# Input projection of a two-layer transformer trunk: chunks in pairs on four accumulators, with seven block products for some K pairs

## The chip, the cores and the metric

The kernel runs on one core of a Trainium2 chip. The metric is the device time of one execution in microseconds (us). The kernel before takes 2220.35 us, the median of 3 runs (2220.18 to 2223.35).

## The reference

Two layers, 256 tokens, width 2048, all float32:

```python
for l in range(DEPTH):
    h = rms_norm(x, pre_mix_norm[l])
    # hybrid_mixer: proj = h @ w_in[l]          (2048 -> 6144)
    #   columns: stick-breaking q, k, v (8 heads x 128),
    #            differential q, k (8 x 2 x 64), v (8 x 128)
    #   A: stick-breaking attention, RMSNorm per head
    #   B: differential attention (two softmax maps, partial rotary on q and k), RMSNorm per head
    #   mix = concat(A, B);  m = mix @ w_o[l]    (2048 -> 2048)
    x = x + rms_norm(m, post_mix_norm[l])
    h = rms_norm(x, pre_ffn_norm[l])
    f = (silu(h @ w_gate[l]) * (h @ w_up[l])) @ w_down[l]   # 2048 -> 5632 -> 2048
    x = x + rms_norm(f, post_ffn_norm[l])
```

## The kernel before

Tokens lie on the 128 partitions in NT = 2 tiles (t = 0, 1). Every weight matrix is cut into chunks of CW = 512 columns and into K pairs (`kp`), that is 2 x 128 rows; one K pair of one chunk is a weight tile of 128x1024 float32, 512 KB. All weight tiles form one stream (`weight_order`), which `fetch` loads on SyncE's queue in that order into "raw" buffers (4 of them), and `feed` splits on the way: ScalarE (ACT) rounds to `hi` (L229), VectorE (DVE) subtracts to `lo` (L231), 6 buffers each. `weights(i, ahead)` keeps the split LOOKAHEAD = 4 tiles ahead of use. The activations are held split too (`xT`, or `xI` in layer 1: one tile per 128 rows, two halves). A **product** of a 128x128 block of activations with a 128x512 block of weights is three matmuls: hi x hi, hi x lo, lo x hi (`unit`, L414 to L416; `product`, L774 to L776).

The stages of a layer are input projection, attention, output projection, gate/up and down projection. In the input projection, `mixer_in` goes through 12 chunks one by one. A chunk takes 2 of the 4 PSUM banks of tag "acc", one for each token tile; the next chunk takes the other two. Chunk number c stands for `kind, g = divmod(c, 2)`: kinds 0, 1, 2 are q, k, v of the stick-breaking heads, kinds 3, 4, 5 those of the differential heads, g is the half of the heads. The order is 6, 8, 10, 7, 9, 11, then 0, 2, 4, 1, 3, 5: the differential heads first. The output projection then reads the mixed heads in the order of `KP_O`, again the differential ones first, and waits with `run_until` for the ones that it needs. When a chunk is done, ACT scales it by the inverse RMS `rs` into `tok` or `v`; POOL rotates differential q and k; `flip` transposes tok on TensorE (PE) through a bank of tag "b" (3 banks), and DVE copies it out (L748). Then `diff_weights` or `stick_weights` compute the attention weights through "b" banks, and `attend` multiplies them with v in the one bank of tag "o". These are generators; `tick()`, called at the start of each group of matmuls, lets them take their next step, so attention's instructions fall between matmuls of the projection. `run_until` ticks until a condition holds. Above that, a scheduler orders each engine's instructions by priority and expected readiness; `tc.high_priority(offset=URGENT)` moves a part forward.

Layer 0 begins with `opening`: x arrives transposed in 8 loads (`xr`), is scaled, split into `xT`, and used at once. `settle` then loads x again, in token order, for its mean squares (`inv_rms`), and loads the small constants (`late_constants`). Layer 1's `xT` is written by the end of layer 0: the down projection's last three K pairs run token tile by token tile, and `rescale` transposes x column group by column group.

Gate/up and down already use **seven products** for some K pairs (`seven_products`; of gate/up's 8, the list SEVEN = 2, 4, 5, 6): the 2x2 block product of (2 token tiles x 2 row blocks) with (2 row blocks x 2 chunks) takes 8 products when done directly; with sums of the operands prepared beforehand it takes 7, four of them into extra banks (`four_banks`), whose contents `shared_part` combines (one ACT copy, four DVE adds). The sums of the weights are made by `mixed_weights`: the tile `T` gets one sum from an accumulating DMA of POOL's queue (`summed`, L191), then DVE makes three adds (L210 to L212) and splits all of it (L206: lo, and Tl in two parts, one 128x512 and one 128x1024). The sums of the activations are made by `token_sums`, from the pair's plain values `f`.

Of the kernel before, what the change touches and what calls it, by code (L numbers as in the profile page):

```python
# [9 lines left out]
F32 = mybir.dt.float32  # L10
# [7 lines left out]
P = 128  # L18
# [12 lines left out]
DEFER = 8  # L31
# [3 lines left out]
KP_O = (4, 5, 6, 7, 0, 1, 2, 3)  # L35
SEVEN = (2, 4, 5, 6)
# [15 lines left out]
def weight_order():  # L52
# [8 lines left out]
    sevens = set()  # L61
    for l in range(L):
        lay = {"in": {}, "o": {}, "gate": {}, "up": {}, "down": {}}
        chunks = []
        for g in range(2):
            chunks += [6 + g, 8 + g, 10 + g]
        for g in range(2):
            chunks += [g, 2 + g, 4 + g]
        lay["chunks"] = chunks
# [21 lines left out]
    return order, plan, sevens  # L91
# [14 lines left out]
class Rooms:  # L106


    LASTING = ("gpost", "t2", "x", "qk")

    def __init__(self, tc, name):
        self.lasting = tc.alloc_tile_pool(name=f"{name}_lasting", bufs=6, reuse_waits="tile")
        self.passing = tc.alloc_tile_pool(name=f"{name}_passing", bufs=6, reuse_waits="tile")

    def tile(self, *args, **kw):
        return (self.lasting if kw["tag"] in self.LASTING else self.passing).tile(*args, **kw)

    def release(self):
        self.passing.release()
        self.lasting.release()  # L120
# [3 lines left out]
def kernel(  # L124
# [35 lines left out]
    order, plan, sevens = weight_order()  # L160
# [35 lines left out]
    def mixed_weights(i):  # L196
# [10 lines left out]

        split(hi, lo, u)
# [10 lines left out]
    def feed(upto):  # L219
        fetch(upto)  # L220
        while fed[0] < min(upto, len(stream)):
            i = fed[0]
            raw = raws[i]
            if i in sevens:
                ready[i] = mixed_weights(i)
                fed[0] += 1
                continue
# [145 lines left out]
    def inv_rms(t, pool, nm):  # L373
        ss = small.tile([P, 1], F32, tag="ssx", name=f"ssx_{nm}_{t}")
        part = small.tile([P, 4], F32, tag="ssp", name=f"ssp_{nm}_{t}")
        for h in range(4):
            junk = pool.tile([P, CW], F32, tag="t2", name=f"junk_{nm}_{t}_{h}")
            nc.scalar.activation(junk, x_part(t, h * CW, CW), AF.Square, accum_out=part[:, h : h + 1])
# [7 lines left out]
    running = []  # L386

# [63 lines left out]
    def norm_pair(pool, ob, mix, mixed, h0, gcol, nm):  # L451
# [10 lines left out]
        )  # L462
        yield
        yield
        for j in range(2):
            mix[h0 + j] = pool.tile([P, 2, S], F32R, tag="mix", bufs=KT, name=f"mix_{nm}_{j}")
# [38 lines left out]
    def stick_weights(pool, l, g, st):  # L505
        q, k = st["q"], st["k"]
        for hp in range(2):
            nm = f"sb{l}_{g}_{hp}"
            za, zb = bank(f"za_{nm}"), bank(f"zb_{nm}")
# [36 lines left out]
            w = pool.tile([P, 2 * (S + P)], F32, tag="w", bufs=3, name=f"w_{nm}")  # L546
            nc.scalar.activation(w[:, 0 : 2 * S], za, AF.Exp)
            nc.scalar.activation(w[:, 2 * S : 2 * S + S], zb[:, 0:S], AF.Exp)
            yield
            yield  # L550
# [7 lines left out]
    def diff_weights(pool, l, g, st):  # L558
        q, k = st["q"], st["k"]
        for hp in range(2):  # L560
            w = pool.tile([P, 2 * (S + P)], F32, tag="w", bufs=3, name=f"pT_{l}_{g}_{hp}")
            for j in range(2):
                h = 2 * hp + j
                nm = f"df{l}_{g}_{h}"
                sc = [bank(f"s{m}_{nm}") for m in range(2)]
                for qt in range(2):
                    for m in range(2):
                        r = slice(m * 64, (m + 1) * 64)
                        nc.tensor.matmul(
                            sc[m][:, qt * P : qt * P + (qt + 1) * P],  # L570
                            q[r, h, qt * P : (qt + 1) * P],
                            k[r, h, 0 : (qt + 1) * P],
                            start=True,
                            stop=True,
                        )
                mx = small.tile([P, 4], F32, tag="mx", name=f"mx_{nm}")
                for m in range(2):
                    blk = sc[m][0:64, 0 : S + S].rearrange("p (b c) -> p b c", c=64)[:, 1:6:4, :]
                    nc.vector.memset(blk, NEG)
                    for qt in range(2):  # L580
                        nc.vector.tensor_reduce(
                            out=mx[:, 2 * qt + m : 2 * qt + m + 1],
                            in_=sc[m][:, qt * P : qt * P + (qt + 1) * P],
                            axis=AX.X,
                            op=ALU.max,
                            negate=True,
                        )
                yield
                e = pool.tile([P, 2, S + P], F32, tag="a", bufs=2, name=f"e_{nm}")
                sm = small.tile([P, 4], F32, tag="sm", name=f"sm_{nm}")  # L590
                for m in range(2):
                    for qt in range(2):
                        c = 2 * qt + m
                        nc.scalar.activation(
                            e[:, m, qt * P : qt * P + (qt + 1) * P],
                            sc[m][:, qt * P : qt * P + (qt + 1) * P],
                            AF.Exp,
                            bias=mx[:, c : c + 1],
                            accum_out=sm[:, c : c + 1],
                        )  # L600
# [37 lines left out]

    def opening(pool, accs, xT):

        first = plan[0]["chunks"][0]

        xr = []

# [451 lines left out]
```

## Time and profile before

| | |
|---|---|
| median of 3 runs | 2220.35 us (2220.18 to 2223.35) |
| profiled execution | 2224.29 us, its span 2222.6 us |
| granted TensorE clock, mean | 0.997 |
| busy: PE / DVE / ACT / POOL | 2197.2 / 1790.0 / 1307.7 / 135.1 us |
| input projection, layer 0 | matmuls from 6.1 to 308.2 us |
| input projection, layer 1 | matmuls from 1107.8 to 1410.5 us |
| DMA | 464.65 MB, mean 209 GB/s |

The profile is of one execution. Busy time of PE is the time in which at least one matmul is under way; matmuls overlap, so it is not the sum of their durations. The granted clock is TensorE's, 1.00 being full speed. A wait is given as the engine and line that waited, and what ended the wait.

### The profile page before, as it was taken

The numbers are of one execution on the slowest core, as the hardware profiler recorded it, in microseconds if no ns is written. First come the engines' busy times: TensorE is split into PE (matmuls) and PEld (weight loads), VectorE is DVE, ScalarE is ACT, GpSimd is POOL, SyncE is SP. The second block draws the span as 40 slices with busy tenths as digits, with TensorE's granted clock in tenths as the row PEclk, the third lists the DMA queues.
The fourth block names the chain that finished last, engine by engine and source line by source line (L and its number), as shares of the span: only waits on it lengthen the run. The fifth ranks groups of instructions, "written<-read, shape, count | busy, mean of one in ns | idle before, by whom it ended". The sixth has DMA issues, their size and how long they took to land.

```text
span 2222.6 us, 28460 instructions
## 1 busy us (share of the span) xinstructions
PE 2197.2 (99%) x10057; PEld 1803.2 (81%) x10057; DVE 1790.0 (81%) x2531; ACT 1307.7 (59%) x1937; POOL 135.1 (6%) x184
## 2 busy tenths in 40 slices
PE   9999999999999999999999999999999999999998
PEld 7888888778888888888888888887788888878886
DVE  6666555899999998989876665559999999989897
ACT  6555554656656656656665455547566556566663
POOL 1200000000100000000010000000000000000000
PEclk9999999999999999999999999999999999999999
DMA  8555455777776675767464655558677677667673
GB/s 287 193 164 168 161 186 184 253 223 229 225 250 213 215 251 186 242 211 243 156 220 166 195 170 169 183 187 271 203 220 238 223 223 235 223 200 240 199 256 99
DMA packets 136783, 464.65 MB, mean 209 GB/s; under 512 B 15680, under 2 KB 16192, under 8 KB 136128
## 3 DMA queue, kind: packets, MB, share of 16 engines
q1 hardware_dynamic: 119216, 428.20, 56.0%
q0 software_dynamic: 15552, 28.32, 7.6%
q10 hardware_dynamic: 1872, 6.31, 0.7%
q8 instruction: 79, 1.29, 0.2%
q14 instruction: 64, 0.52, 0.1%
HBM read 454.38 MB, written 8.39 MB: 208 GB/s over the span
## 4 chain that ended last, share of the span: by engine, by line
PE 87%; DVE 7%; issue 2%; DMA 2%; ACT 2%; SPq 0%; DVEq 0%; ACTq 0%
PE c L774 8%; PE c L775 8%; PE c L776 8%; PE in L414 8%; PE in L416 8%; PE in L415 8%; PE dn L980 5%; PE dn L981 5%; PE dn L983 5%; PE o L416 3%; PE o L415 3%; PE o L414 2%; PE p L775 2%; PE p L774 2%; PE p L776 2%
## 5 line engine op out<-in xcount | busy, mean ns | idle before, releaser
L231 DVE TENSOR_TENSOR lo<-raw,hi 128x1024 fp32r<-128x1024 f32 x567 | 687.3, 1225 | 240.2 <-ACT hi L229 236.0
L229 ACT ACTIVATE hi<-raw 128x1024 fp32r<-128x1024 f32 x567 | 592.1, 1055 | 389.1 <-PE in L416 160.2
L774 PE MATMUL c<-hi,xF 128*128 128x512 f32 x820 | 321.8, 396 | 6.4 <-DVE w L815 2.9
L776 PE MATMUL c<-hi,xF 128*128 128x512 f32 x820 | 320.0, 392 | 0.0
L775 PE MATMUL c<-lo,xF 128*128 128x512 f32 x820 | 319.9, 391 | 0.0
L191 POOL DMA_DIRECT2D T<-in_weights_in_turn_dram x108 | 94.1, 871 | 1715.7 <-DMA T<-in_weights_in_turn_dram 540.4
L774 PEld LDWEIGHTS c<-hi,xF 128*128 128x128 f32 x820 | 154.0, 188 | 41.1 <-DVE w L815 4.1
L980 PE MATMUL dn<-hi,jh 128*128 128x512 f32 x464 | 180.8, 390 | 0.0
L776 PEld LDWEIGHTS c<-hi,xF 128*128 128x128 f32 x820 | 154.4, 188 | 32.4
L981 PE MATMUL dn<-lo,jh 128*128 128x512 f32 x464 | 180.6, 389 | 0.0
L775 PEld LDWEIGHTS c<-lo,xF 128*128 128x128 f32 x820 | 154.6, 189 | 30.8
L414 PE MATMUL in<-hi,xT 128*128 128x512 f32 x384 | 154.1, 402 | 1.6 <-ACT hi L229 1.6
L414 PE MATMUL in<-hi,xI 128*128 128x512 f32 x384 | 153.9, 401 | 0.2 <-ACT xI L355 0.2
L231 DVE TENSOR_TENSOR lo<-G,hi 128x1024 fp32r<-128x1024 f32 x108 | 131.6, 1219 | 26.5 <-ACT hi L229 26.4
L415 PE MATMUL in<-lo,xT 128*128 128x512 f32 x384 | 150.5, 392 | 0.5 <-DVE lo L231 0.5
L416 PE MATMUL in<-hi,xT 128*128 128x512 f32 x384 | 150.9, 393 | 0.0
L416 PE MATMUL in<-hi,xI 128*128 128x512 f32 x384 | 150.5, 392 | 0.1
L415 PE MATMUL in<-lo,xI 128*128 128x512 f32 x384 | 150.0, 391 | 0.5 <-DVE lo L231 0.5
L983 PE MATMUL dn<-hi,jl 128*128 128x512 f32 x464 | 142.9, 389 | 0.0
L205 ACT ACTIVATE Th<-T 128x512 fp32r<-128x512 f32 x108 | 67.7, 627 | 127.5 <-DVE T L210 127.1
L206 DVE TENSOR_TENSOR lo<-T,hi 128x1024 fp32r<-128x1024 f32 x108 | 131.6, 1219 | 12.3 <-ACT hi L205 12.2
L206 DVE TENSOR_TENSOR Tl<-G,Th 128x1024 fp32r<-128x1024 f32 x108 | 131.7, 1220 | 10.1 <-ACT Th L205 10.1
(310 smaller groups left out, 4310.4 us busy)
## 6 DMA issues: line engine op xcount, KB each, us to landing
raw<-in_weights_in_turn_dram SPq DMA_DIRECT2D x567, 512.0 KB, 4.3
T<-in_weights_in_turn_dram SPq DMA_DIRECT2D x108, 512.0 KB, 4.3
G<-in_weights_in_turn_dram SPq DMA_DIRECT2D x108, 512.0 KB, 4.6
T<-in_weights_in_turn_dram POOLq DMA_DIRECT2D x108, 256.0 KB, 6.7
away_ffn<-x ACTq DMA_DIRECT2D x8, 512.0 KB, 7.0
xd<-away_ffn SPq DMA_DIRECT2D x8, 512.0 KB, 10.3
xr<-in_x_columns_dram SPq DMA_DIRECT2D x8, 256.0 KB, 6.7
x<-in_x_dram SPq DMA_DIRECT2D x4, 512.0 KB, 8.2
```

Source lines behind the costliest of these rows:

```text
L206: nc.vector.tensor_tensor(out=l, in0=w, in1=h.bitcast(F32), op=ALU.subtract)
L229: nc.scalar.activation(hi, raw, AF.Copy)
L231: nc.vector.tensor_tensor(out=lo, in0=raw, in1=hi.bitcast(F32), op=ALU.subtract)
L414: nc.tensor.matmul(a, sh, hi[:, kk, :], start=first and kk == 0, stop=False)
L415: nc.tensor.matmul(a, sh, lo[:, kk, :], start=False, stop=False)
L416: nc.tensor.matmul(a, sl, hi[:, kk, :], start=False, stop=last and kk == 1)
L774: nc.tensor.matmul(a, sh, hi, start=first, stop=False)
L775: nc.tensor.matmul(a, sh, lo, start=False, stop=False)
L776: nc.tensor.matmul(a, sl, hi, start=False, stop=last)
L980: nc.tensor.matmul(accs[c, t], sh, hi[:, kk, :], start=first, stop=False)
L981: nc.tensor.matmul(accs[c, t], sh, lo[:, kk, :], start=False, stop=False)
L983: nc.tensor.matmul(accs[c, t], sl, hi[:, kk, :], start=False, stop=last)
```

## The change

- The 12 chunks go in 6 pairs (`PAIRS`). A pair's two chunks are computed together, K pair by K pair, on all four "acc" banks (`eight_in`: 8 products, 24 matmuls). The first and the last K pair of a pair of chunks go token tile by token tile, and after each half of the last one `settle(t)` reads two banks, with priority.
- K pairs listed in `IN_NOW` use seven products (`seven_in`), in one burst per pair of chunks: none in layer 0's first pair, 5 and 6 in layer 1's first, 4, 5, 6 in the second, 4 and 5 in the three after it, none in the last. The extra banks are the three "b" and the one "o", which attention uses otherwise. `IN_ORDER` puts the K pairs 0, 1 ahead of the burst and 2, 3, 7 behind it.
- Attention steps that take such banks start only if they end before the next burst (`clear(n)`), and one at a time (`claims`); `diff_weights` runs as two generators, one for each j.
- For these tiles the first weight sum is made by DVE on tiles loaded plainly (`plain`), not by an accumulating DMA.
- In layer 0 the opening does a pair of chunks, x for the mean squares is loaded beside it (`first_stats`), and the token sums of K pairs 4, 5, 6 are made beside it too. In layer 1 they are made during the first pair of chunks.
- The copies out of `flip` and of the transposed differential weights move from DVE to ACT. The pools are laid out anew; x for the residual is loaded in the last pair.

```diff
-DEFER = 8
+PAIRS = ((6, 8), (10, 7), (9, 0), (11, 2), (1, 3), (4, 5))
+IN_SEVEN = (4, 5, 6)
+IN_ORDER = (0, 1, 4, 5, 6, 2, 3, 7)
+IN_NOW = tuple((first, (4, 5, 6), (4, 5), (4, 5), (4, 5), ()) for first in ((), (5, 6)))
...
-        for c in chunks:
-            for kp in range(KT // 2):
-                lay["in"][c, kp] = queue_pair("w_in", l, kp, c)
+        for n, (ca, cb) in enumerate(PAIRS):
+            for kp in IN_ORDER if n else range(KT // 2):
+                lay["in"][ca, kp] = queue_pair("w_in", l, kp, ca)
+                lay["in"][cb, kp] = queue_pair("w_in", l, kp, cb)
+                if kp in IN_NOW[l][n]:
+                    plain.add(lay["in"][cb, kp])
...
+        if i in plain:
+            nc.vector.tensor_tensor(out=u[:, 0, :], in0=g[:, 0, :], in1=u[:, 0, :], op=ALU.add)
         split(hi, lo, u)
...
+    def clear(n):
+        return burst[0] is None or clock[0] + n <= burst[0]
...
         for hp in range(2):
-            while (hp, 1) not in st["w"] or "v" not in st:
+            while (hp, 1) not in st["w"] or "v" not in st or claims[1] or not clear(4):
                 yield 1
+            claims[1] += 1
...
-                nc.vector.tensor_copy(wj, tp[:, 0 : S + P])
+            nc.scalar.copy(wj, tp[:, 0 : S + P])
...
         for kp in range(KT // 2):
             if kp:
                 split(2 * kp)
                 split(2 * kp + 1)
-            if kp + 4 < KT // 2:
+            if kp + 2 < KT // 2:
                 load()
-                fetch(kp + 5)
-            unit(accs, xT, plan[0]["in"][first, kp], kp, range(NT), kp == 0, kp == KT // 2 - 1, 0)
+                fetch(2 * kp + 6)
+            for part in ((0,), (1,)) if kp == KT // 2 - 1 else (range(NT),):
+                eight_in(accs, xT, 0, PAIRS[0], kp, part, kp == 0, kp == KT // 2 - 1, 0)
+                if kp == KT // 2 - 1:
+                    settle(part[0])
+            if 3 <= kp < 7:
+                next(stats)
+            if kp >= 4 and kp - 4 < len(IN_SEVEN):
+                sums_of(IN_SEVEN[kp - 4])
...
+    def eight_in(accs, xT, l, cc, kp, toks, first, last, ahead=LOOKAHEAD):
+        ws = [weights(plan[l]["in"][c, kp], ahead) for c in cc]
+        for kk in range(2):
+            for t in toks:
+                tick()
+                st = xT[2 * kp + kk]
+                stat = (st[:, 0, t * P : (t + 1) * P], st[:, 1, t * P : (t + 1) * P])
+                for col, (hi, lo) in enumerate(ws):
+                    product(accs[2 * t + col], stat, (hi[:, kk, :], lo[:, kk, :]), first and kk == 0, last and kk == 1)
...
+        for n, cc in enumerate(PAIRS):
+            banks = [acc_bank(f"in{l}_{c}_{t}") for t in range(NT) for c in cc]
+            mine = IN_NOW[l][n]
+            w, toks = None, {}
+            def settle(t):
+                with tc.high_priority(offset=URGENT):
+                    for col, c in enumerate(cc):
+                        kind, g = divmod(c, 2)
+                        src = banks[2 * t + col]
+                        if w is not None:
+                            src = w[:, 2 * t + col, :]
+                            nc.vector.tensor_tensor(out=src, in0=banks[2 * t + col], in1=src, op=ALU.add)
...
+                        nc.scalar.activation(tok, src, AF.Copy, scale=rs[t][:, by : by + 1])
...
+                    if n == 0 and 2 <= j < 2 + len(IN_SEVEN):
+                        sums_of(IN_SEVEN[j - 2])
+                    if kp in mine:
+                        if extra is None:
+                            extra = four_banks(True, [f"{q}_in{l}_{n}" for q in ("p1", "p6", "p7", "q5")])
+                        seven_in(banks, extra, forms[kp], xT, l, cc, kp, kp == mine[0], kp == mine[-1])
+                        if kp == mine[-1]:
+                            burst[0] = None
+                            w = pool.tile([P, 4, CW], F32, tag="gpost", bufs=1, name=f"w{l}_{n}")
+                            shared_part(extra, [w[:, i, :] for i in range(4)])
...
+                    if first or last:
+                        for t in range(NT):
+                            eight_in(banks, xT, l, cc, kp, (t,), first, last)
+                            if last:
+                                settle(t)
+                    else:
+                        eight_in(banks, xT, l, cc, kp, range(NT), first, last)
```

More of the change, by code (lines that the diff above doesn't have):

```diff
@@ L637, in rotate, with opening @@
         eng.tensor_tensor(out=v16, in0=ra, in1=rb, op=ALU.add)
-    def opening(pool, accs, xT):
-        first = plan[0]["chunks"][0]
+    def opening(pool, accs, xT, stats, sums_of, settle):
         xr = []
```

380 lines of the change are left out of this document (222 added, 158 removed).

## The prediction

> **What bounds the kernel now.** I read the page's busy shares first, then the chain of waits and TensorE's own waits, then the time by stage, and last the first microseconds instruction by instruction.
>
> ```profile
> PE 2197.2 (99%) x10057; PEld 1803.2 (81%) x10057; DVE 1790.0 (81%) x2531; ACT 1307.7 (59%) x1937; POOL 135.1 (6%) x184
> ...
> PE   9999999999999999999999999999999999999998
> ...
> DVE  6666555899999998989876665559999999989897
> ...
> PE 87%; DVE 7%; issue 2%; DMA 2%; ACT 2%; SPq 0%; DVEq 0%; ACTq 0%
> ```
>
> TensorE (PE) is busy everywhere and carries 87% of the chain. VectorE (DVE) has a hole just where the change works: tenths 5 and 6 at the start and in the middle, which are the two input projections (0 to 308 us and 1107 to 1410 us), and nines elsewhere. The same by stage, in windows of 40 us (columns: stretch, length, busy us and instructions of PE, weight load, DVE, ACT, POOL, then clock, DMA share, GB/s):
>
> ```profile
> 60.00:100.00 40.00, 40.00 (x201) 31.96 (x200) 26.13 (x46) 19.17 (x35) 1.93 (x2) 1.00 0.60 200
> 260.00:300.00 40.00, 40.00 (x196) 33.46 (x195) 20.84 (x25) 18.98 (x29) 0.00 (x0) 1.00 0.58 197
> 460.00:500.00 40.00, 38.28 (x171) 30.76 (x169) 37.88 (x48) 23.86 (x29) 3.46 (x4) 1.00 0.66 200
> 600.00:640.00 40.00, 40.00 (x182) 33.06 (x181) 37.56 (x44) 23.72 (x28) 3.48 (x4) 1.00 0.72 234
> ```
>
> The first two are input projection: DVE 52 to 65%. The last two are gate/up, which has seven products already: DVE at 94% and PE without a gap once settled (600), but 1.7 us of PE lost in 40 while a backlog of DVE is being worked off (460). These two are my scale for the changed stage. PE's waits in the whole run are few:
>
> ```profile
> PE c L774 <- DVE w L815: 2.9, 2, 1.8
> PE p_d L775 <- DVE Tl L206: 2.0, 2, 1.7
> PE in L414 <- ACT hi L229: 1.6, 1, 1.6
> PE in L415 <- DVE lo L231: 1.1, 2, 0.5
> ```
>
> So the prices are: an instruction less on PE is worth its spacing, and an instruction more on DVE is free until it makes PE late. The spacing, and the one weak place of the input projection, are in PE's timeline (start, us, engine, line):
>
> ```profile
> 8.80 0.39 PE L416 MATMUL in<-hi,xT 128*128 128x512 f32 x1
> 10.79 0.73 PE L414 MATMUL in<-hi,xT 128*128 128x512 f32 x2 [1.59 <-ACT hi L229]
> 12.04 0.50 PE L415 MATMUL in<-lo,xT 128*128 128x512 f32 x1 [0.53 <-DVE lo L231]
> 13.48 0.63 PE L414 MATMUL in<-hi,xT 128*128 128x512 f32 x1
> 13.90 0.63 PE L415 MATMUL in<-lo,xT 128*128 128x512 f32 x1
> 20.35 0.39 PE L415 MATMUL in<-lo,xT 128*128 128x512 f32 x1
> 20.58 0.39 PE L416 MATMUL in<-hi,xT 128*128 128x512 f32 x1
> ```
>
> Matmuls start 0.2265 us apart (20.35 to 20.58; 29 of them from 17.40 to 23.98), although each lasts 0.39 us: the spacing counts, not the duration.
>
> **Part 1, fewer matmuls.** The list IN_NOW marks 9 K pairs in layer 0 and 11 in layer 1. Each does 7 block products in place of 8, and a product is 3 matmuls: 20 x 3 = 60 fewer; PE's instruction order of the changed kernel has 2244 matmuls of the input projection against 2304. 60 x 0.2265 = 13.6 us, all on the path. That is the ceiling of this part: **-13.6 us**.
>
> **Part 2, the opening.** Between 8.80 and 16.02 us only 12 matmuls run after the one at 8.80: 7.0 us for 2.7 us of work, 4.3 us lost, 2.1 us of it waiting for the second weight tile and 2 us because matmuls then come 0.43 us apart (the granted clock of 10 to 15 us is 0.76). With two chunks at a time a K pair feeds PE 24 matmuls (5.44 us) for 1.25 MB in place of 12 (2.72 us) for 0.75 MB. By the order of the loads, the second K pair's weights stand 0.5 to 1 MB later in the queue; at 320 to 400 GB/s (5 to 15 us) that is some 2 us later, when PE has 2.7 us more to do. I take 1.8 us lost instead of 4.3: **-2.5 us**, between 0 and -4.
>
> **Part 3, DVE's load.** Counted from the order of both kernels, over two layers: 20 Tl of 128x1024 (1.220) and 20 of 128x512 (0.684), 80 adds on raw tiles (the three that the gate/up helper has, plus the one that a DMA of POOL does there; 0.686), 36 adds of shared_part and 36 of settle (0.686), 6 token-sum sets (2 x 0.419 + 4 x 0.285 + 0.683 = 2.66): 24.4 + 13.7 + 54.9 + 49.4 + 16.0 = 158 us. Off DVE go 32 flip copies (0.686) and 16 pT copies (0.554), 31 us, to ACT, which is below 65% here. Net +127 us, 64 a layer. DVE was busy 191 us of layer 0's first 308 (sum of the windows), so it comes to about 255 of 301, 85%. Below the 94% at which gate/up runs without gaps: on the average this costs PE nothing. It costs where load is bunched.
>
> In a burst a seven needs eight DVE operations (2 lo, 4 adds, 2 Tl), 7.1 us of durations, or 6.3 us back to back (the next start follows a 128x1024 after 1.13, 1116.21 to 1117.34 us, and a 128x512 after 0.60, 1106.59 to 1107.19), and PE uses it up in 21 x 0.2265 = 4.76 us. A burst of three is 4.6 us short, one of two 3.1 us. The cover is the lead: hi and lo have 6 buffers, Th and Tl 2, so two K pairs are ready ahead, and an eight gives back 3.2 us (5.44 less 2 x 1.13). Gate/up does kp 4, 5, 6 in a row under the same cover. I cost bursts in the middle at nothing; without the lead they are the first rival.
>
> **Part 4, layer 1's first pair.** Here the load is bunched. In the trace of before DVE is full there with rescaling and transposing x, 4.6 to 5.0 of each 5 us from 1105 to 1125. The change puts behind that three token-sum sets, two sevens, shared_part and four settling adds. From the order, back to back from 1130.5 us (where the old kernel's eighth weight tile is done): the second seven's last Tl comes at about 1155, and ten of the pair's matmuls wait for it, 2.3 us more: 1157.5. PE alone would be done at 1155.5 (the old second chunk ended at 1156.9, less 6 matmuls). Then shared_part and settle end at about 1163, while PE has only 14 matmuls on the one bank already free: another 2.5 us. With half a microsecond for the next seven: **+5 us**, between 0 (the DVE sum is 5% off, or the next pair fills the gap) and 9.
>
> **Part 5, the handovers.** Four accumulators are all that the "acc" tag has, so a pair can't start until the last one is read out: 6 handovers a layer, where before two of the four were free. Covered by the split by tokens: the last K pair ends t=0 first, and its 2 banks are read (2 x 0.686) while 12 matmuls of t=1 run, 2.72 us. What DVE has just begun can cost up to 1.23 more: 2.6, still covered; one more op queued in front costs 0.5. Priority URGENT puts the reads in front. For ten of them I take 0.2 each, **+2 us**, between 0 and 8. What queues behind a late read on DVE are the next pair's lo and Tl, which have the lead.
>
> A stall can also slow the clock: after the 2.1 us of waiting at 9 to 12 us ten matmuls came 0.43 us apart, 2 us lost, while gate/up's wait of 1.8 us left the clock at 1.00. One such slow stretch in part 4 is inside its bound of 9. The page "TensorE: Matmul & The Clock Gate" of the Trainium skill (Part 1: The HAM clock gate) halves the clock only after an idle window of about 3.4 us once it is warm; by it part 4 would bring none.
>
> The handover out of layer 0's opening is another matter: rs now is computed beside it (8 squares of x on ACT behind 2 MB of loads), the lambda loads stand ahead of the next pair's weights on SP's queue, and lprod waits for them on DVE ahead of that pair's lo. Those loads take 1.3 us each on SP (32.5 to 37.7 us before). The 12.5 MB ahead of them take 39 us at 320 GB/s from 2.5, so the last x lands near 42, the weights near 47, and PE needs them at 50. **+1.5 us**, between 0 and 4.
>
> **Part 6, attention and the rest.** Same matmuls, same softmax. Steps wait for bursts to pass; PE's order shows them spread between in-projection matmuls and all scores done before the output projection, whose first 21.8 us read only differential heads (KP_O) while four reads of the stick-breaking group (some 5.5 us each) run beside. If they were late, PE would wait at the first sb K pair. 0, between -1 and 2.
>
> Sum: -13.6 - 2.5 + 5 + 2 + 1.5 = **-7.6 us**. The profiled execution took 2224.3 (span 2222.6 and 1.7 around it), 3.9 above the median of 2220.35; so 2216.7 there and **2212.7** as a median. A measurement of this kernel tells about 0.2%, 4.4 us, from no change: faster is below 2215.9, slower above 2224.8.
>
> **The rivals.**
> *The lead fails (slower).* If every seven is paced by DVE, since attention's DVE steps stand between its eight operations, each costs 6.3 - 4.76 = 1.55 us: 31 us, and with parts 1, 2 and 5 alone it is 2220.35 - 16.1 + 31 + 3.5 = 2239. It decides when DVE's share in a pair nears 95%; by my sums the pairs in the middle have 41 to 44 us of 46 to 48, 90 to 92%; from 12.6 of its 31 us on the sign turns. For: 460 to 500 us. Against: 600 to 640 us. Chance of an outcome slower than 2224.8: 0.20.
> *Handovers uncovered.* PE waits at each for two reads, 1.4 us, 12 times: 17 us in place of the 8.5 of parts 4 and 5, so 2220.35 - 16.1 + 16.8 = 2221. For: no second set of banks. Against: at the end of layer 0 the down projection's four banks pass to the next layer in the same order by tokens, and PE waited 0.2 us (1107.84). 0.13, as a result within 0.2%. The page "Perfetto Trace Analysis" of the Trainium skill (Matmuls) asks that independent groups rotate through PSUM banks, so that the reading of one overlaps the next one's matmuls; by that rule this rival is what comes.
> *All stalls vanish.* The scheduler fills layer 1's gap: -16.1 and 2 lost, 2206. 0.17.
> *My forecast*, 2207 to 2216: 0.50. That the matmuls aren't gone is excluded by the order.
>
> Faster 0.67, same 0.12, slower 0.21. The range leaves out about a tenth at each side: from 2203 (2220.35 - 13.6 - 4, the bounds of parts 1 and 2 with no stall) to 2227 (the first rival with 19 of its 31 us).
>
> **What would show it.** Right: in-projection PE count 2244; no wait of PE over 1 us from 60 to 300 us and from 1175 to 1400; DVE 80 to 92% there; PE idle of 4 to 6 us between 1145 and 1165, released by DVE Tl and w; second K pair of the opening about 2 us late at most. Wrong: many waits of about 1.5 us on Tl in each burst (first rival), waits on w or tok at each pair's first matmul (second), PE stalled at mix_sb, or gate/up later than its shift.

## The result, and the profile after

The changed kernel takes 2232.93 us, the median of 4 runs (2231.65 to 2235.65), beside 2220.54 for the kernel before in the same comparison: ratio 1.0055, 95% interval 1.0037 to 1.0072. It is 12.4 us slower; 2212.7 was forecast, 7.6 us faster. The two profiled executions lie 9.7 us apart (2233.99 and 2224.29), since the one before was 3.8 us above the median of 2220.54 and the one after 1.1.

First the page of the changed kernel: busy times, tenths of PE and DVE, and the chain's shares.

```profile
PE 2192.2 (98%) x9997; PEld 1790.3 (80%) x9997; DVE 1896.3 (85%) x2718; ACT 1363.4 (61%) x2041; POOL 137.6 (6%) x184
...
PE   9999999999999999999989999999999999999998
...
DVE  7888655899999998989899886558999999989897
...
PE 77%; DVE 13%; DMA 4%; issue 3%; ACT 2%; SPq 0%; DVEq 0%; ACTq 0%
```

The 60 matmuls are gone (x9997 against x10057). DVE has 106 us more; its first four tenths are 7 8 8 8 in place of four sixes. But PE has an 8 in the middle, where layer 1's input projection begins, and ten points of the chain have left PE, most of them for DVE and DMA. By stage (columns as before; the last row is layer 1's first pair and the beginning of the second):

```profile
60.00:100.00 40.00, 38.28 (x179) 28.98 (x178) 35.82 (x55) 26.18 (x44) 0.46 (x1) 1.00 0.58 186
260.00:300.00 40.00, 40.00 (x194) 33.45 (x193) 19.34 (x19) 21.97 (x31) 0.00 (x0) 1.00 0.56 184
1140.00:1200.00 60.00, 52.97 (x222) 39.59 (x220) 53.16 (x69) 34.55 (x42) 12.33 (x16) 0.97 0.50 160
```

In 60 us PE loses 7.0 us with DVE at 89%, less than the 94% at which gate/up ran without a gap. PE's waits (engine, line, what it waited for, then us in total, times, longest):

```profile
PE in L903 <- DVE w L794: 3.4, 1, 3.4
PE p_in L903 <- ACT Th L221: 2.7, 2, 1.6
PE qkT_ps L823 <- ACT qT L824: 2.5, 2, 1.3
PE oT_ps_df L499 <- DVE w L941: 2.3, 2, 1.2
...
PE q_in L903 <- ACT hi L221: 1.1, 1, 1.1
```

L794 is settle's add, L941 to L944 are the four adds of `shared_part`, L221 and L222 the split in `mixed_weights`, L247 and L249 the split of a plain tile, L823 and L824 the transposes of `flip` and their copy, L499 the transposes of an attention output. Two of the five are the sevens' own sums; qkT_ps and oT_ps_df are attention's transposes, for which the prediction had set nothing.

The account of the difference comes from the matmuls' start times: whatever lies between two starts beyond 0.2265 us is a gap, and the gaps above 0.34 us are put down to what stands behind them.

| in the profiled executions, us | forecast | measured |
|---|---|---|
| 60 matmuls less | -13.6 | -13.6 |
| opening, and the first matmul at 6.79 in place of 6.09 | -2.5 | -2.4 + 0.7 |
| layer 1's first pair, handover out of it included | +5 | +8.9 |
| the other handovers, and the one out of layer 0's opening | +3.5 | 0 |
| the other sevens' waits for Th, Tl and hi | 0 | +3.8 |
| attention's steps behind bursts (4.3 in layer 0, 3.4 in layer 1) | 0 | +7.7 |
| gaps under 0.34 us in the input projections | - | +2.4 |
| attention's work that moved from output to input projection | 0 | +0.6 |
| gate/up and down projection | 0 | +1.1 |
| sum | -7.6 | +9.2 |

The last matmul of the down projection starts at 2221.96 against 2212.70, 9.3 us later.

How one of the new waits comes about is in the timeline of 124 to 130 us, just behind a burst, first of PE, then of ACT:

```profile
127.53 0.40 PE L903 MATMUL in<-hi,xT 128*128 128x512 f32 x1
129.24 0.63 PE L823 MATMUL qkT_ps<-ident,tok 128*128 128x128 f32 x4 [1.32 <-ACT qT L824]
...
127.57 1.06 ACT L247 ACTIVATE hi<-raw 128x1024 fp32r<-128x1024 f32 x1 [1.46 <-DMA raw<-in_weights_in_turn_dram]
128.53 0.57 ACT L824 COPY qT<-qkT_ps 128x512 f32<-128x512 f32 x1
```

The burst ended at 124.7, and attention's steps, held back until then, come at once: by 126 us a score has two of the three "b" banks and a first flip the third. The second flip needs that one; its copy stands on ACT behind a split whose weight tile has not landed, and PE, which has other matmuls behind the transpose, stands still for 1.3 us. The waits of oT_ps are of the same kind on DVE, where shared_part's add, which frees the bank, stands behind a lo.

### The profile page after: what moved, and what is told of

It is laid out like the page before. It is cut to its first block, busy times and chain, and to the rows that moved or that the text cites. A ratio compares the mean times of both kernels' runs of the same rounds, so it can differ in the third digit from the quotient of the medians.

```text
span 2232.3 us, 28660 instructions
## 1 busy us (share of the span) xinstructions
PE 2192.2 (98%) x9997; PEld 1790.3 (80%) x9997; DVE 1896.3 (85%) x2718; ACT 1363.4 (61%) x2041; POOL 137.6 (6%) x184
## 4 chain that ended last, share of the span: by engine, by line
PE 77%; DVE 13%; DMA 4%; issue 3%; ACT 2%; SPq 0%; DVEq 0%; ACTq 0%
PE c L904 8%; PE c L905 8%; PE c L903 8%; PE in L903 5%; PE in L905 5%; PE in L904 5%; PE dn L1109 4%; PE dn L1110 4%; PE dn L1112 4%; DMA raw<-in_weights_in_turn_dram 4%; DVE lo L249 4%; PE o L441 3%; PE o L443 3%; PE o L442 3%; PE p L903 2%
## 5 line engine op out<-in xcount | busy, mean ns | idle before, releaser
L249 DVE TENSOR_TENSOR lo<-raw,hi 128x1024 fp32r<-128x1024 f32 x546 | 657.7, 1223 | 164.8 <-ACT hi L247 163.9
L247 ACT ACTIVATE hi<-raw 128x1024 fp32r<-128x1024 f32 x546 | 565.5, 1053 | 254.0 <-DMA raw<-in_weights_in_turn_dram 75.5
L249 DVE TENSOR_TENSOR lo<-G,hi 128x1024 fp32r<-128x1024 f32 x108 | 131.7, 1220 | 27.8 <-ACT hi L247 27.7
L221 ACT ACTIVATE Th<-T 128x512 fp32r<-128x512 f32 x108 | 67.6, 626 | 128.0 <-DVE T L228 128.0
L222 DVE TENSOR_TENSOR lo<-T,hi 128x1024 fp32r<-128x1024 f32 x108 | 131.7, 1220 | 12.1 <-ACT hi L221 11.5
L222 DVE TENSOR_TENSOR Tl<-G,Th 128x1024 fp32r<-128x1024 f32 x108 | 131.7, 1220 | 9.3 <-ACT Th L221 9.2
L221 ACT ACTIVATE hi<-T 128x1024 fp32r<-128x1024 f32 x108 | 113.3, 1049 | 42.3 <-PE c L905 25.1
L221 ACT ACTIVATE Th<-G 128x1024 fp32r<-128x1024 f32 x108 | 113.9, 1054 | 39.1 <-DVE G L230 38.9
L903 PE MATMUL in<-hi,xT 128*128 128x512 f32 x321 | 128.2, 401 | 0.3 <-ACT xT L695 0.3
L903 PE MATMUL in<-hi,xI 128*128 128x512 f32 x307 | 123.3, 405 | 4.4 <-DVE w L794 3.4
L904 PE MATMUL in<-lo,xT 128*128 128x512 f32 x321 | 125.9, 392 | 0.7 <-DVE lo L249 0.7
L905 PE MATMUL in<-hi,xT 128*128 128x512 f32 x321 | 125.7, 392 | 0.0
```

What stands on the lines that cost most here:

```text
L221: nc.scalar.activation(h, w, AF.Copy)
L222: nc.vector.tensor_tensor(out=l, in0=w, in1=h.bitcast(F32), op=ALU.subtract)
L247: nc.scalar.activation(hi, raw, AF.Copy)
L249: nc.vector.tensor_tensor(out=lo, in0=raw, in1=hi.bitcast(F32), op=ALU.subtract)
L903: nc.tensor.matmul(a, sh, hi, start=first, stop=False)
L904: nc.tensor.matmul(a, sh, lo, start=False, stop=False)
```

## The experiments

Ratios are to the kernel before, run beside each kernel. "In 0" and "in 1" are the stretches in the profile from the first matmul of a layer's input projection to the first of its output projection, in us. They are of one execution each, which for one_seven lay 9.2 us above the kernel's median and for first_plain 5.7; differences of a microsecond between them tell little.

| kernel | ratio (95%) | in 0 | in 1 |
|---|---|---|---|
| before | 1 | 302.4 | 302.9 |
| changed | 1.0055 (1.0037 to 1.0072) | 302.7 | 312.1 |
| pairs_only | 1.0001 (0.9993 to 1.0010) | 300.4 | 303.6 |
| first_plain | 1.0037 (1.0025 to 1.0049) | 302.0 | 307.2 |
| copies_dve | 1.0060 (1.0048 to 1.0073) | 303.0 | 313.4 |
| light_sums | 0.9983 (0.9974 to 0.9992) | 297.3 | 304.0 |
| spaced | 1.0067 (1.0055 to 1.0079) | 302.6 | 316.4 |
| one_seven | 1.0022 (1.0013 to 1.0031) | 303.1 | 307.6 |
| raw6 | 1.0081 (1.0068 to 1.0094) | 300.7 | 305.5 |
| raw5_lo5 | 1.0060 (1.0047 to 1.0072) | 301.2 | 307.8 |
| pool_add | 1.0125 (1.0112 to 1.0138) | 309.0 | 322.4 |
| hold4 | 1.0022 (1.0012 to 1.0031) | 298.3 | 309.2 |
| urgent_shared | 1.0047 (1.0034 to 1.0059) | 302.7 | 310.8 |
| pairs_load | 1.0034 (1.0022 to 1.0047) | 306.2 | 306.2 |
| hold_plain | 1.0002 (0.9993 to 1.0010) | 298.1 | 303.4 |
| hold_sixteen | 0.9980 (0.9971 to 0.9989) | 298.9 | 300.0 |
| hold8_sixteen | 0.9963 (0.9950 to 0.9975) | 297.8 | 297.7 |
| hold_late | 0.9993 (0.9983 to 1.0003) | 298.9 | 303.7 |

### Pairs or sevens

**pairs_only.**

```diff
-IN_NOW = tuple((first, (4, 5, 6), (4, 5), (4, 5), (4, 5), ()) for first in ((), (5, 6)))
+IN_NOW = ((),) * 6, ((),) * 6
```

> No K pair with seven products: the chunks still go in pairs on four accumulators, with the new opening, the handovers and the copies on ACT, but all 2304 matmuls of the input projection are back and no burst takes attention's banks. Three theories. (A) The pairs themselves are sound and every loss comes with the sevens (their DVE work, the weight tiles that they hold, the banks that they take): then the waits of PE on attention's steps, on Tl and on w all go, and the time is the one before less what the opening gains, 2.4 us, plus 0.7 for the later first matmul: 2218 to 2221. (B) Attention's waits (4.3 us in layer 0, 3.4 in layer 1) come from the copies that moved to ACT, where they queue behind splits that wait for a load, sevens or not: then they stay and it is 2225 to 2228. (C) The handovers on four accumulators cost: waits at each pair's first matmul, 12 of them, above 2228.

Ratio 1.0001, and in its profile no gap above 0.38 us in either input projection from 55 us on, but for the ones at 1107 to 1116 us that the kernel before has as well. So pairs on four accumulators, the handovers and the copies on ACT cost nothing by themselves; the opening's gain is seen in the profile (in 0 is 2.0 us shorter) and not in the medians. The 12.4 us, and the 13.6 us of matmuls saved, are all lost with the sevens: about 26 us for 20 of them.

**copies_dve.** `nc.scalar.copy` becomes `nc.vector.tensor_copy` in `flip` and `diff_weights`.

> The copies out of flip and of the transposed differential weights go back from ACT to DVE (48 copies, 31 us of DVE), all else as in the changed kernel. If attention's transposes wait because their copies queue on ACT behind a split whose weight tile has not landed (theory B), the waits of qkT_ps on qT (1.3 us in each layer) and of s_df on kT (0.6) go: 2229 to 2230. If DVE is the engine that lacks time (theory A), 31 us more on it make the bursts worse: 2235 to 2240. If the late weight tile holds up DVE's queue in the same way, the waits only change their name: 2232 to 2234.

1.0060, no different from the changed kernel, and in 0 and in 1 are longer by 0.3 and 1.2 us. qkT_ps waits less, s_df and the first pair's splits wait instead. Which engine copies is not the cause.

### DVE's time, or the sevens' chain

**light_sums.**

```diff
-        nc.vector.tensor_tensor(out=t2, in0=u[:, 0, :], in1=t2, op=ALU.add)
-        nc.vector.tensor_tensor(out=g[:, 0, :], in0=t2, in1=g[:, 0, :], op=ALU.subtract)
-        nc.vector.tensor_tensor(out=g[:, 1, :], in0=t2, in1=g[:, 1, :], op=ALU.add)
+        if i not in plain:
+            ...
```

> Three of the four weight sums of each of the input projection's 20 sevens are left out (60 adds of DVE, 0.6 us each, 36 us; the sevens then work on wrong operands, and their matmuls, splits, loads and banks are the same). If DVE's work in a burst is what makes PE late (theory A), a seven now needs 4.5 us of DVE beside 4.8 of PE: the waits on Tl, Th and w inside bursts go (3.8 us in the middle pairs) and most of the 8.9 us of layer 1's first pair: 2222 to 2225. If it is the weight tiles that arrive late behind a burst because the four raw buffers are held (theory C), they are held 1.8 us a seven shorter only: attention's waits stay in part, 2226 to 2230. If neither, 2233.

The kernel leaves out three of the four weight sums. 0.9983: 16 us faster than the changed kernel for 36 us of DVE, more than expected. These adds stand between the landing of two weight tiles and the splits to Th and Tl; without them the chain is shorter too, not only DVE's load. The next kernel has load alone.

**pairs_load.**

```diff
+                    if kp in LOADED[l][n]:   # the K pairs that are sevens in the changed kernel
+                        for _ in range(7):
+                            nc.vector.tensor_tensor(out=other[1], in0=other[0], in1=other[0], op=ALU.add)
```

> The kernel with pairs but without any seven (ratio to before 1.0001) gets DVE work that nothing waits for: at each K pair that is a seven in the changed kernel, seven adds of 128x512 into a tile that is never read (140 adds, 4.2 us for each K pair, 84 us in all, about what a seven adds to DVE). No raw tile is held, no bank is taken, no sum is waited for. If DVE's load as such makes PE late (theory A), it loses what the sevens lose, 1.2 us for each: ratio 1.008 to 1.012. If load is harmless with the lead of two K pairs, and it is what a seven holds (raw tiles, banks) or its chain of steps that costs, 1.000 to 1.002.

1.0034, between the two: 84 us of unattached adds cost 7.3 us against pairs_only, 0.09 us for each, where the 36 us inside the sevens were worth 0.44 each. The adds did not stay at the sevens' K pairs, since nothing holds them there: in the trace all 63 of layer 0 lie before 115 us and all 77 of layer 1 between 1129 and 1247 us, while PE works on the changed kernel's sevens until 225 and 1338 us. So this is load alone, but crowded to the front. Two stretches of this kernel:

```profile
60.00:100.00 40.00, 38.21 (x185) 29.39 (x184) 39.55 (x75) 20.27 (x43) 7.56 (x8) 0.96 0.56 184
1140.00:1200.00 60.00, 60.00 (x285) 48.33 (x284) 58.24 (x87) 28.67 (x45) 14.56 (x16) 1.00 0.59 192
```

From 1140 to 1200 us DVE is at 97%, and PE loses nothing; the changed kernel lost 7.0 us there at 89%. From 60 to 100 us, at 99%, PE loses 1.8 us: at 96 us a score waits for a softmax step on ACT (`e_df`), which had itself waited 3.6 us for DVE. The same happens at 1204 us, and these two places, with the matmuls at half clock behind the first, make up about 6 us of this kernel's gaps. So load alone can make attention's steps late too, but a share of DVE by itself is no measure of what PE loses.

**pool_add.** The `plain` add of `mixed_weights` goes to `nc.gpsimd`.

> The first weight sum of each of the 20 sevens (128x512) is added by POOL, which is busy 6% of the time, in place of DVE: 20 x 0.6 = 12 us off DVE. Leaving 36 us out took 16 us off the time, so 12 are worth up to 5: 2228 to 2229. Against: POOL's adds of 128x128 took 0.56 us here where DVE's 128x512 take 0.69, so one of 128x512 may take 2 us or more on POOL, and hi, lo, Th and Tl of the seven all wait for it: if that delay outweighs DVE's relief, 2233 to 2238.

1.0125, worse than the worst expected. The add by form, and PE's longest wait:

```profile
L225 POOL TENSOR_TENSOR raw<-raw,raw 128x512 f32<-128x512 f32 x20 | 32.0, 1603 | 337.5 <-DMA raw<-in_weights_in_turn_dram 330.9 <-DVE w L794 3.4 <-PE in L905 3.3
...
PE p_in L903 <- ACT Th L221: 8.5, 3, 5.2
```

The add takes 1.60 us on POOL where DVE took 0.69, so each seven's chain is 0.9 us longer although DVE has 12 us less to do: 16 us lost. In its profile some 5 us of that are matmuls at half clock behind longer waits (34 matmuls 0.43 us apart in the two stretches, 8 in the changed kernel). Together with light_sums it shows that the chain counts: what stands between a tile's landing and the last Tl.

### Bunching, number and buffers

**spaced.** `IN_ORDER` is (0, 1, 4, 2, 5, 3, 6, 7).

> Only the order of the K pairs changes, from 0 1 4 5 6 2 3 7 to 0 1 4 2 5 3 6 7: between two sevens of a burst stands a K pair with eight products, in which DVE has 2.3 us of work beside 5.4 of PE. Work on every engine stays the same. Shown so far: leaving 36 us of DVE out of the sevens takes 16 us off. Theory 1, the bunching: a seven is 1.5 us short of DVE, three in a row use up the lead of two K pairs; with an eight between, 3.1 us are given back and the waits behind bursts (sevens 3.8 us, attention's steps 7.7 us, none of them in the pairs without sevens) mostly go: 2224 to 2227, layer 1's first pair (8.9 us) being untouched. Theory 2, the average: DVE has too much in a pair of chunks as a whole, wherever it stands: 2231 to 2234. A cost of spacing: attention's banks are taken for five K pairs rather than three, which delays its steps; if they come late, PE waits in the output projection and it is slower than the changed kernel.

1.0067: not better, so three sevens in a row are not by themselves what hurts. The waits for Th stay (3.6 us in three), and the extra banks are taken for five K pairs: a score waits 2.2 us for w at 1346 us.

**one_seven.** `IN_NOW` has (4,) in the four middle pairs and nothing else.

> One seven only (K pair 4) in each of the four middle pairs of both layers, none in layer 1's first pair: 8 sevens in place of 20, 24 matmuls fewer than before in place of 60 (5.4 us against 13.6). The price for each pair of chunks that has any seven, shared_part and the adds in settle, is paid eight times against ten. Theory 1 (bunching): a single seven is covered by the lead, nothing waits: pairs alone took what the kernel before takes, so 2222.5 - 5.4 = 2217, ratio to before 0.9975. Theory 2 (the average): DVE's load falls by 12 sevens of 3.9 us net each and the losses fall in proportion, from 25 us for 20 sevens to 10 for 8: 2222.5 + 10 - 5.4 = 2227. If it is a price for each pair of chunks (banks taken from attention, settle), losses stay near 8/10 of theirs: above 2232.

1.0022, or 2227.55 us: against theory 1, and the number of theory 2 (2227). Eight single sevens lose 4.9 + 5.4 = 10 us, 1.3 each, as much as in bursts. That the loss goes with the number of sevens does not show that DVE's time is the reason: the largest wait is a transpose that asks for a bank of the burst just ended. PE, then DVE, around 1177 us:

```profile
1174.64 0.60 PE L823 MATMUL qkT_ps<-ident,tok 128*128 128x128 f32 x4
1177.50 1.06 PE L823 MATMUL qkT_ps<-ident,tok 128*128 128x128 f32 x4 [2.26 <-DVE w L941]
...
1173.68 1.23 DVE L249 TENSOR_TENSOR lo<-raw,hi 128x1024 fp32r<-128x1024 f32 x1 [1.89 <-ACT hi L247]
1175.52 1.23 DVE L249 TENSOR_TENSOR lo<-raw,hi 128x1024 fp32r<-128x1024 f32 x1 [0.62 <-ACT hi L247]
1176.67 0.68 DVE L941 TENSOR_TENSOR w<-p_in,w 128x512 f32<-128x512 f32 x1
```

DVE is idle for 0.6 us ahead of the second lo, which waits for ACT, while the add that would free the bank stands behind it in the queue. This is a wait for order, not for DVE's time.

**raw6** (raw 6 buffers, hi and lo 5 each) and **raw5_lo5** (raw 5, lo 5).

> Raw buffers 6 in place of 4, hi and lo 5 each in place of 6 (the same memory): weight tiles can land two earlier, and the split can be one tile less ahead. If the waits behind bursts come from loads that start late because a seven holds two of four raw buffers through eight operations of DVE (theory C; ACT waited 75 us on raw tiles, 61 before), ACT's waits on raw fall below 40 us and attention's waits (7.7 us) go: 2224 to 2227. If DVE's time is what lacks, loads that come earlier find DVE busy, and the shorter lead of hi and lo makes the bursts worse: 2233 to 2240.

> Raw buffers 5 in place of 4, lo 5 in place of 6, hi as it is. With raw 6 and hi, lo 5 the input projections alone were 2.0 and 6.6 us shorter than in the changed kernel, ACT hardly waited for a raw tile there, but the end of layer 0 and the handover into layer 1 lost 11 us. If raw buffers are what the sevens lack (theory C) and the loss elsewhere came from the one tile less of lead, one raw buffer more gives about half of 8.6 us in the input projections and the loss elsewhere stays, since lo is again 5: ratio 1.006 to 1.008 with input projections 4 us shorter. If the loss elsewhere came from the hi buffers, it is gone: 1.003 to 1.004.

Both input projections are shorter than in the changed kernel, by 2.0 and 6.6 us with six and by 1.5 and 4.3 us with five: in layer 0 that points to late weight tiles as a part of the cause. Layer 1's share may only have moved ahead of the stretch, for 10.5 us (raw6) and 3.9 us (raw5_lo5) are lost from layer 0's first down matmul to layer 1's first matmul, 4.3 and 3.5 of them in one wait for the rescaled x, and the ratios are no better (1.0081, 1.0060). Why that end of layer 0 is so much later wasn't settled.

### The banks, and layer 1's first pair

**first_plain.** `IN_NOW[1][0]` is empty.

> Layer 1's first pair of chunks does all its K pairs with eight products (6 matmuls more, 1.4 us); its token sums are still made there, all else as in the changed kernel. If DVE's backlog in that pair is what PE waits for (8.9 us of gaps between 1145 and 1170 us, 1.4 of them at half clock), they go: 2233 - 8.9 + 1.4 = 2225 to 2226. If the backlog is only handed on, because the token sums, rescaling and transposing are what fill DVE, half of it comes back as waits in the second pair: 2229 to 2231. A theory that the loss is spread evenly over all bursts gives 2 of 20 sevens, 2 us at most: 2232.

1.0037: 4 us better, as the second expectation had it. The gaps of 1145 to 1170 us are gone, and the second pair's first seven waits for Tl at 1187 us (1.6 us in the list of waits, 2.1 us between the two starts) with matmuls 0.43 us apart behind it.

**hold4.**

```diff
     def clear(n):
-        return burst[0] is None or clock[0] + n <= burst[0]
+        return clock[0] >= held[0] and (burst[0] is None or clock[0] + n <= burst[0])
...
                             burst[0] = None
+                            held[0] = clock[0] + 4
```

> After each burst attention's steps that need banks are held back for four more ticks (5.4 us of eights), so that shared_part's adds on DVE have read the extra banks before a transpose asks for one; nothing else changes. In the changed kernel PE waits 7.7 us in the two layers at attention's first steps behind bursts (transposes and scores, released by w's adds on DVE or by copies on ACT). If the wait is for banks that DVE reads late (theory D), most of it goes: ratio to before 1.0055 - 0.0025 = 1.003 or below. If the engines behind the steps are themselves late because weight tiles come late, the steps wait all the same, later: 1.005 to 1.006. Against: attention's tail comes 5.4 us later after every burst and has less room before the next: above 1.006.

1.0022, 7.3 us better than the changed kernel by a hold of four ticks; the expectation was 5.6 or more. Behind bursts one transpose still waits (0.9 us); nothing is lost in the output projection. In 0 is 4.3 us shorter than in the changed kernel and in 1 2.9.

**urgent_shared.** `shared_part` within `tc.high_priority(offset=URGENT)`.

> shared_part (one copy on ACT, four adds on DVE for each burst) is issued with priority, as settle is, so that it stands in front of the following weight tiles' splits on DVE. If the waits behind bursts are for its reads (theory D), PE's waits on w (oT, 2.3 us; c and the first pair's handover, 3.4 us, are settle's) shrink: ratio 1.003 to 1.0045. If what stands in front is itself waiting for a load, or if the splits that are pushed back make the next K pair late, the gain is paid back: 1.005 to 1.007.

1.0047, not to be told from the changed kernel. The first pair's handover waited less (gaps of 0.8 and 1.2 us for one of 3.8), while Th waits grew from 2.7 us to 4.6: the splits pushed back are missed.

**hold_plain** (hold4 with first_plain) and **hold_late** (layer 1's second pair without sevens too).

> Attention's steps held back four ticks behind each burst, and layer 1's first pair without sevens (18 sevens left). Each edit alone took the ratio to before from 1.0055 to 1.0022 and to 1.0037. If they act on different waits (attention's steps behind bursts; DVE's backlog in layer 1's first pair) they add: 1.0022 - 0.0018 = 1.0004, no different from before. If both only shift one backlog, 1.002.

> Attention's steps held back four ticks; layer 1's first two pairs have no sevens at all, layer 0 keeps its nine (15 sevens left). If layer 1's loss is the backlog of its first pair (rescaling, transposing and token sums on DVE, then sevens), it is gone by the third pair and all gaps from 1140 to 1200 us go: against hold_plain 4.5 us less of gaps for 2.0 us of matmuls, ratio 0.999. If the sevens of layer 1 cost the same wherever they stand, 1.000 to 1.001.

hold_plain 1.0002: the two edits add within the interval (1.0004 was expected), as two separate causes would. hold_late 0.9993, an interval that holds 0.999 as well as 1.000. In its profile the gaps from 1140 to 1200 us are gone, but in 1 is as long as in hold_plain: behind the first burst that is left an o_df waits 2.0 us for w, with matmuls at half clock after it.

**hold_sixteen** and **hold8_sixteen.**

```diff
+IN_NOW = (((), (5, 6), (4, 5), (4, 5), (4, 5), ()),) * 2
...
+                            held[0] = clock[0] + 4    # 8 in hold8_sixteen
```

> As hold_plain, and the second pair of both layers has the sevens 5 and 6 alone in place of 4, 5, 6: four K pairs with eight products stand ahead of its burst, and 16 sevens are left (1.4 us more on PE). In layer 1 the backlog of the first pair reached the second pair's sevens (4.5 us of gaps with first_plain), which have 2.7 us more of lead here; in layer 0 the first burst waited 1.4 us for Th. If that wait is a backlog that time works off, 4 to 5 us go for 1.4: ratio 0.998 to 0.999, faster than both kernels. If each seven has its price (1.2 us less 0.7), 0.9998.

> As hold_sixteen, with eight ticks held in place of four. With four, one transpose still waited for a copy on ACT 3 us behind a burst (1.2 us in layer 0), when two of shared_part's four adds were not done. If eight cover shared_part wholly: 1 to 2 us better than hold_sixteen. If attention's steps then run into the next burst, or come late for the output projection, 2 us worse or more.

0.9980 and 0.9963: faster than both kernels, the second by 6.6 us in the medians (2215.84 against 2222.40); the intervals of the two overlap, so what eight ticks add to four is less sure. K pair 4 now has eight products, so that three K pairs of eights stand ahead of the second pair's sevens in place of two (the expectation counts four), and the wait of layer 1's first sevens is gone. One window of the changed kernel's layer 0, then hold8_sixteen's windows of layer 0 and of layer 1:

```profile
60.00:300.00 240.00, 235.46 (x1142) 189.31 (x1142) 187.94 (x302) 152.72 (x277) 10.00 (x17) 1.00 0.55 180
...
60.00:300.00 240.00, 238.03 (x1164) 193.66 (x1163) 182.82 (x296) 152.59 (x275) 12.39 (x20) 1.00 0.56 186
1140.00:1200.00 60.00, 60.00 (x277) 49.24 (x277) 44.78 (x55) 33.51 (x41) 10.08 (x18) 1.00 0.68 220
```

From 60 to 300 us DVE does 182.8 us, hardly less than in the changed kernel (187.9), and PE loses 2.0 us against 4.5, with 16 sevens for 20. What makes the sevens pay is when the banks are asked for and how much lead the first seven of a pair finds.

## Why the prediction was wrong, step by step

- **Part 1** was right: 2244 matmuls, 13.6 us.
- **Part 2** was right: 1.9 us lost in the opening where 1.8 were forecast. The wait is now for a lo, half way through a K pair:

```profile
12.80 0.39 PE L903 MATMUL in<-hi,xT 128*128 128x512 f32 x1
13.94 0.50 PE L904 MATMUL in<-lo,xT 128*128 128x512 f32 x1 [0.75 <-DVE lo L249]
```

- **Part 3** failed at "I cost bursts in the middle at nothing". DVE's work was sized well enough (127 us forecast as a sum of durations, 131 measured; durations overlap, and DVE's busy time rose by 106 us, to 78% of 60 to 300 us where 85% was forecast). The step from share to cost was wrong. It took 94% in gate/up as the point up to which DVE is free, but pairs_load had 97% over 60 us without a gap, and the changed kernel lost 7.0 us of 60 at 89% and 4.5 us of 240 at 78%. The lead of two K pairs is not full here: before, ACT's splits waited 73.5 us of 60 to 300 us for PE to free a hi buffer; in the changed kernel 12.6, and 15.1 for a tile that had not landed. Outside layer 1's first pair the sevens' waits cost 3.8 us.
- **Part 4** named the right place, sums and order, and was mis-sized: 8.9 us for 5, just inside its bound of 9, with 1.4 us of it at half clock behind the longest wait. The seven's Tl, forecast at 1155, ended at 1159, and settle's first add came at 1164.3 because it has to follow shared_part's first add, whose operand it overwrites, and both stood between splits that waited for tiles. The timeline of PE and DVE there:

```profile
1161.36 0.39 PE L905 MATMUL in<-hi,xI 128*128 128x512 f32 x1
1165.16 0.47 PE L903 MATMUL in<-hi,xI 128*128 128x512 f32 x1 [3.41 <-DVE w L794]
...
1161.30 1.23 DVE L249 TENSOR_TENSOR lo<-raw,hi 128x1024 fp32r<-128x1024 f32 x1 [1.03 <-ACT hi L247]
1162.44 0.68 DVE L941 TENSOR_TENSOR w<-p_in,w 128x512 f32<-128x512 f32 x1
1163.18 1.23 DVE L249 TENSOR_TENSOR lo<-raw,hi 128x1024 fp32r<-128x1024 f32 x1
1164.33 0.68 DVE L794 TENSOR_TENSOR w<-in,w 128x512 f32<-128x512 f32 x1
```

- **Part 5** was too high: in the changed kernel no other handover has a gap over 0.34 us, and pairs_only has none at all. Here 12 matmuls of the other token tile cover two reads. The rule of the Trainium skill that it was weighed against ("Perfetto Trace Analysis", Matmuls: rotate the banks) did not decide.
- **Part 6** failed, by 7.7 us, the largest miss of the sum. It asked whether attention would be late for the output projection (it was not) and not what its first steps behind a burst wait for. They come all at once, and for 5 us the reads that free their banks (shared_part's adds, the steps' own copies) queue on DVE and ACT behind splits that wait for weight tiles; PE, whose next matmuls stand behind these steps, waits with them. hold4 took most of it away.

The steps that failed in parts 3, 4 and 6 are together 15.4 us (3.8, 3.9 and 7.7): they alone turn the forecast of -7.6 us into +7.8, where the account above has +9.2.

Of the rivals, "the lead fails" gave the sign and nearly the time (2239; its terms, though, are not what was measured: its point of decision, a DVE share near 95%, is not borne out by pairs_load (nothing lost at 97% over 60 us, 1.8 us at 99% over 40) nor by the changed kernel (7.0 us at 89%), and the waits behind bursts were no part of it). Its own spacings add up to 6.4 us a seven in place of 6.3, which makes it 1.6 us and some 2241. That the loss per seven was 1.3 us where it had 1.55 is chance: less than half of it is sevens waiting for their own sums.

Open: the end of layer 0 with other buffers (raw6). Gate/up of layer 0 took 469.9 us in the profile before, 471.6 after and 471.7 without sevens; the difference is nearly all half clock, for 8 and 7 matmuls came 0.43 us apart there, 1.6 and 1.4 us, and none in the kernel before. Over all the profiles that stretch took 469.9 to 476.2 us, with 0 to 20 such matmuls.

## What to carry to other kernels

Price work on a helper engine by the chain it lengthens and by what stands behind it in that engine's queue, not by its share of busy time alone: 84 us of unattached adds, crowded to the front, cost 7 us here, and leaving out 36 us inside the sevens' chain gained 16. When a burst borrows banks, count when each is read out in the queue as it stands, and keep the next user away until then: a hold of eight ticks and four sevens fewer turned 12 us lost into 6.6 gained. Work on a chain should not be moved to an idle engine that does it in 1.60 us in place of 0.69.

## What the runs showed of the hardware

A wait of PE can cost more than itself. In gate/up of layer 0 PE waited 1.85 us and 0.22 before it, and from 429 us the granted clock was halved. PE's timeline and the windows of that stretch:

```profile
425.14 0.74 PE L903 MATMUL c<-hi,xF 128*128 128x512 f32 x2 [0.22 <-ACT hi L247]
427.73 0.50 PE L904 MATMUL c<-lo,xF 128*128 128x512 f32 x1 [1.85 <-DVE lo L249]
...
429.72 0.63 PE L905 MATMUL c<-hi,xF 128*128 128x512 f32 x1
430.14 0.63 PE L904 MATMUL c<-lo,xF 128*128 128x512 f32 x1
...
429.00:432.50 3.50, 3.50 (x10) 2.72 (x9) 3.50 (x6) 0.00 (x0) 0.00 (x0) 0.52 0.84 279
```

Matmuls came 0.43 us apart for about 3.5 us, some 1.6 us lost on top of the wait. The length of a wait does not settle it. Behind the 1.61 us wait at 1147 us matmuls kept their 0.23 us, and in copies_dve the same two waits of gate/up (0.22 and 1.85 us, 425 and 428 us) left the clock at 1.00. In first_plain a wait of 1.27 us (1237 us) was followed by matmuls 0.43 us apart. The kernel before has such a stretch too: behind the 1.83 us wait of gate/up in layer 1 (1603 us) the clock was 0.53 for 3.5 us, so the prediction's reading that gate/up's wait of 1.8 us left it at 1.00 was wrong.

The Trainium skill ("TensorE: Matmul & The Clock Gate", Part 1: The HAM clock gate) has the clock halved after an idle window of about 3.4 us; here waits of 1.3 to 1.9 us were enough in some places and not in others, so the measurement decides, and a price for a wait of more than 1.3 us should allow for both outcomes.
